# Windowed attention in fp32: the output stores moved onto the queue of the loads, with a reordered TensorE stage

## The chip, the cores and the metric

The kernel runs on one core of one Trainium2 chip. The metric is the device time of one execution in microseconds (us). TensorE is PE, VectorE DVE, ScalarE ACT, GpSimd POOL, SyncE SP. Transfers run on 16 DMA engines: in the traces the semaphore of each transfer of 128 partitions gets 16 completion counts, whether GpSimd or SP issued it. The time from the first to the last of the 16 is called the spread below; a large spread means that some DMA engines lag behind the others. A transfer issued by GpSimd goes onto GpSimd's queue (q0 in the profile), one issued by SP onto SP's (q1). The runs of a kernel scatter by about 1 us, so differences below half a microsecond are not read.

## The reference, cut to what matters

```python
B, S, D, W = 4, 4096, 1536, 64             # q, k, v: fp32, B x S x D
logits = einsum('bnwd,bnud->bnwu', q_w, k_w) * D ** -0.5   # in windows of 64 rows
attn = softmax(logits)
out  = einsum('bnwu,bnud->bnwd', attn, v_w)                # fp32
```

There are 16,384 rows of 1,536 numbers in each tensor. The core must read 302 MB and write 101 MB of HBM whatever it does on chip.

## The kernel before

Work goes in units of 256 rows: 63 of them, then two of 128. In a unit, partition p holds two consecutive rows of the tensor, so each partition's share of a transfer is one contiguous piece of 12,288 bytes. I call such a piece a row from here on. Loads are issued by GpSimd and cast fp32 to fp16 on the way; stores are issued by SP, but for the last few.

```python
    def load(u):
        for name, src in (("q", qf), ("k", kf), ("v", vf)):
            t = inp.tile([P, LR, D], FP16, tag=name + "16", name=name + "16")
            ...
            nc.gpsimd.dma_start(out=dst, in_=dram(src, u))
    ...
    def store(i):
        u = units[i]
        src = ...
        eng = nc.gpsimd if i >= N - PREFETCH - 2 else nc.sync
        eng.dma_start(out=dram(of, u), in_=src)

    prev = None
    for i, u in enumerate(units):
        if i + PREFETCH < N:               # PREFETCH = 3
            load(units[i + PREFETCH])
        for g in range(u.G):
            et = finish_scores(scores(u, g))
            if prev is not None:           # values one unit behind the scores
                pi, pg, pet = prev
                values(units[pi], pg, pet, False)
                ...
                    store(pi)
            prev = (i, g, et)
    ...
    values(units[pi], pg, pet, True)       # its three stores go to SP
```

`scores` transposes q and k on PE into PSUM and copies the result to SBUF (half the copies on DVE, half on ACT), then multiplies and exponentiates. `values` multiplies with v, and scales by the row sums while it evacuates PSUM into `out_sb`.

The build adds a limit: GpSimd's transfers share eight completion semaphores, so each waits for the eighth before it, and eight are in flight at most.

The softmax here doesn't subtract the row's maximum and nothing guards it: scores larger than these inputs give would overflow.

## Time and profile before

| | before |
|---|---|
| median of 4 runs | 958.65 us (958.32 to 959.07) |
| span of the profiled run | 956.8 us |
| first data packet starts, last ends | 2.6 us, 953.1 us |
| SP has seen every transfer complete | 953.6 us |
| GpSimd's final drain ends | 956.1 us |

Lines of the page of the kernel before. The first gives each engine's busy time, its share of the span and its instructions. The second has the busy share of the DMA engines in 40 slices, in tenths. Then come the queues with packets, MB and the time of their packets as a share of 16 engines' span, and the chain of waits that ended last, by engine.

```profile
PE 658.4 (69%) x5624; PEld 482.7 (50%) x5624; DVE 240.6 (25%) x392; ACT 456.1 (48%) x705; POOL 105.8 (11%) x204
...
DMA  9999999999999999999999999999999999999996
...
q0 software_dynamic: 28656, 156.51, 78.0%
q1 hardware_dynamic: 9072, 95.16, 24.0%
q8 instruction: 44, 0.72, 0.3%
...
HBM read 301.99 MB, written 100.66 MB: 421 GB/s over the span
...
DMA 86%; PE 8%; ACT 4%; issue 1%; DVE 0%; POOL 0%; ACTq 0%; POOLq 0%; DVEq 0%
```

No compute engine is near its limit, the DMA engines are busy in every slice, and the chain of waits runs through transfers. The shares of q0 and q1 add to over 100% because one packet's start overlaps the end of the one before. Loads count with their fp16 size in MB here; in HBM they are twice that.

The windows view of the kernel before: start and end in us, length, busy us of each engine (with instructions), granted PE clock, DMA share, GB/s.

```profile
100.00:500.00 400.00, 282.07 (x2373) 208.07 (x2371) 101.13 (x162) 191.78 (x298) 42.83 (x82) 0.87 1.03 267
500.00:900.00 400.00, 277.06 (x2382) 202.23 (x2380) 101.13 (x162) 192.31 (x298) 42.78 (x81) 0.89 1.03 267
925.00:940.00 15.00, 12.32 (x119) 8.68 (x118) 4.92 (x9) 9.37 (x15) 0.53 (x1) 0.94 0.99 267
940.00:957.00 17.00, 5.70 (x51) 3.12 (x49) 3.62 (x7) 7.03 (x12) 1.06 (x2) 0.81 0.61 250
```

A DMA share of 1.03 through the middle means that the engines are always busy. Each engine carries 2,048 rows.

```profile
SPq L257 <- PEq L257: 3.1, 2, 2.6
```

GpSimd issues its last store at 947.9 us. SP, having seen every transfer complete, waits 2.6 us longer at the closing barrier. The instruction records of the trace (not shown in the page's busy times) say for whom: a drain instruction of GpSimd that runs from 947.8 to 956.1 us.

### The profile page before, as it was taken

How to read it: one execution, taken by the hardware profiler on the slowest of the kernel's cores; microseconds unless marked ns; L12 is line 12 of the kernel's file. 1: busy time of each engine (PE TensorE's matmuls, PEld its weight loads, DVE VectorE, ACT ScalarE, POOL GpSimd, SP SyncE). 2: the span in 40 equal slices, each digit the busy share in tenths (PEclk: the TensorE clock that was granted, in tenths of full speed). 3: DMA queues.
4: the chain of work that ended last, by engine and by line, in shares of the span. 5: the costliest groups of instructions: out<-in, count | busy, mean ns of one | idle time of the engine just before them, and what ended most of it. 6: DMA issues, size and time to landing. Idle time of an engine off the chain costs nothing.

```text
span 956.8 us, 13110 instructions
## 1 busy us (share of the span) xinstructions
PE 658.4 (69%) x5624; PEld 482.7 (50%) x5624; DVE 240.6 (25%) x392; ACT 456.1 (48%) x705; POOL 105.8 (11%) x204
## 2 busy tenths in 40 slices
PE   4776766767767677676776766767667667676674
PEld 3454554645545555455464554555545445445452
DVE  1222222222222222222222222222222222222222
ACT  2544545444445454454545544445445444454445
POOL 3111011110110111101111011011110111111000
PEclk9978889888898898888978989889988999898888
DMA  9999999999999999999999999999999999999996
GB/s 185 242 268 263 275 269 258 279 258 269 270 256 279 257 270 279 250 277 267 259 280 255 271 272 255 279 259 269 279 252 275 266 261 279 257 269 273 253 252 268
DMA packets 37786, 252.51 MB, mean 264 GB/s; under 512 B 4192, under 2 KB 4192, under 8 KB 29664
## 3 DMA queue, kind: packets, MB, share of 16 engines
q0 software_dynamic: 28656, 156.51, 78.0%
q1 hardware_dynamic: 9072, 95.16, 24.0%
q8 instruction: 44, 0.72, 0.3%
q14 instruction: 14, 0.11, 0.0%
HBM read 301.99 MB, written 100.66 MB: 421 GB/s over the span
## 4 chain that ended last, share of the span: by engine, by line
DMA 86%; PE 8%; ACT 4%; issue 1%; DVE 0%; POOL 0%; ACTq 0%; POOLq 0%; DVEq 0%
DMA k<-in_k_dram 40%; DMA v<-in_v_dram 40%; DMA q<-in_q_dram 6%; PE tp L140 3%; PE lt L165 3%; ACT xt L147 2%; PE o L198 2%; ACT et L177 1%; ACT out_sb L204 1%; DVE xt L145 0%; PE lt L126 0%; PE sp L187 0%; POOL q L84 0%; ACTq L257 0%; POOL v L84 0%
## 5 line engine op out<-in xcount | busy, mean ns | idle before, releaser
L140 PE MATMUL tp<-ident,k 128*128 128x128 f16 x1536 | 259.6, 270 | 172.9 <-DMA k<-in_k_dram 172.9
L147 ACT COPY xt<-tp 128x1024 f16<-128x1024 f16 x192 | 194.3, 1012 | 348.3 <-PE tp L140 348.3
L140 PE MATMUL tp<-ident,q 128*128 128x128 f16 x1536 | 253.6, 264 | 52.1 <-ACT xt L147 21.4
L140 PEld LDWEIGHTS <-k 128*128 128x128 f16 x1536 | 156.8, 125 | 184.0 <-DMA k<-in_k_dram 183.8
L198 PE MATMUL o<-v,et 128*128 128x512 f16 x762 | 185.1, 378 | 61.5 <-ACT out_sb L204 61.4
L145 DVE COPY xt<-tp 128x1024 f16<-128x1024 f16 x192 | 132.7, 691 | 346.5 <-PE tp L140 346.5
L140 PEld LDWEIGHTS <-q 128*128 128x128 f16 x1536 | 163.0, 120 | 97.3 <-issue 67.6
L165 PE MATMUL lt<-xt 128*128 128x256 f16 x1512 | 188.4, 277 | 0.5
L204 ACT ACTIVATE out_sb<-o,rs 128x512 f32<-128x512 f32 x256 | 168.9, 686 | 19.0 <-PE o L198 11.1
L165 PEld LDWEIGHTS <-xt 128*128 128x128 f16 x1512 | 144.6, 100 | 31.2 <-ACT xt L147 13.8
L177 ACT ACTIVATE et<-lt,zeros 32x128 f16<-32x128 f32 (+1 forms) x256 | 91.8, 358 | 124.5 <-PE sp L187 114.6
L198 PEld LDWEIGHTS <-et 128*128 128x128 f16 x762 | 69.0, 96 | 146.9 <-issue 79.2
L206 DVE TENSOR_SCALAR out_sb<-o,rs 128x512 f32<-128x512 f32 x128 | 96.1, 750 | 151.4 <-PE o L198 151.4
L84 POOL DMA_DIRECT2D v<-in_v_dram x65 | 34.4, 529 | 343.1 <-PE o L198 309.9
L84 POOL DMA_DIRECT2D k<-in_k_dram x65 | 34.5, 531 | 332.4 <-DMA v<-in_v_dram 332.4
L192 DVE RECIPROCAL rs<-sp 128x2 f32<-128x2 f32 (+1 forms) x65 | 11.1, 170 | 209.1 <-PE sp L187 209.1
L84 POOL DMA_DIRECT2D q<-in_q_dram x65 | 34.6, 532 | 141.6 <-DMA k<-in_k_dram 140.8
L187 PEld LDWEIGHTS <-et 128*128 128x128 f16 x254 | 15.7, 97 | 1.9 <-ACT et L177 0.5
L187 PE MATMUL sp<-ones,et 128*128 128x1 f16 x254 | 15.6, 164 | 0.1
L216 POOL DMA_DIRECT2D out_dram<-out_sb x4 | 2.1, 532 | 25.2 <-ACT out_sb L204 22.3
L126 PE MATMUL lt<-xt 128*128 128x128 f16 x24 | 2.4, 221 | 2.6 <-ACT xt L147 1.7
L126 PEld LDWEIGHTS <-xt 128*128 128x128 f16 x24 | 1.4, 98 | 3.3 <-ACT xt L147 2.0
(10 smaller groups left out, 3.0 us busy)
## 6 DMA issues: line engine op xcount, KB each, us to landing
out_dram<-out_sb SPq DMA_DIRECT2D x60, 1536.0 KB, 11.4
q<-in_q_dram POOLq DMA_DIRECT2D x63, 768.0 KB, 40.4
k<-in_k_dram POOLq DMA_DIRECT2D x63, 768.0 KB, 38.1
v<-in_v_dram POOLq DMA_DIRECT2D x63, 768.0 KB, 38.0
out_dram<-out_sb POOLq DMA_DIRECT2D x3, 1536.0 KB, 9.1
q<-in_q_dram POOLq DMA_DIRECT2D x2, 384.0 KB, 30.3
k<-in_k_dram POOLq DMA_DIRECT2D x2, 384.0 KB, 26.2
v<-in_v_dram POOLq DMA_DIRECT2D x2, 384.0 KB, 21.9
```

The lines of the kernel that those rows point to most:

```text
L84: nc.gpsimd.dma_start(out=dst, in_=dram(src, u))
L126: nc.tensor.matmul(lv[:, r, :, :], lhsT=xt[:, c, 1, r, :], rhs=xt[:, c, 0, :R, :], start=(c == 0), stop=(c == DC - 1),)
L140: nc.tensor.transpose(tp[:, c - c0, x, r, :], src[:, g * R + r, c * P : (c + 1) * P], ident)
L145: nc.vector.tensor_copy(out=dst, in_=tp)
L147: nc.scalar.copy(out=dst, in_=tp)
L165: nc.tensor.matmul(lv[:, r, :, :], lhsT=xt[:, c, 1, r, :], rhs=xt[:, c, 0, :R, :], start=(c == 0), stop=(c == DC - 1),)
L177: nc.scalar.activation(et[s, :, :, s], lv[s, :, :, s], EXP, bias=zeros[s], scale=scale)
L187: nc.tensor.matmul(sp[:, t, 0:1], lhsT=et[:, r, t, :], rhs=ones[:, 0:1], start=(r == 0), stop=(r == R - 1),)
L192: nc.vector.reciprocal(out=rs, in_=sp[:, :, 0])
L198: nc.tensor.matmul(o, lhsT=et[:, r, t, :], rhs=u.v[:, g * R + r, sl], start=(r == 0), stop=(r == R - 1),)
L204: nc.scalar.activation(dst, o, COPY, bias=0.0, scale=rs[:, t : t + 1])
L206: nc.vector.tensor_scalar_mul(dst, o, scalar1=rs[:, t : t + 1])
```

## The change

Its intent is to have loads and stores pass in one order through one queue, to let the q transposes run while k still loads, to run the values right behind the scores, and to give the transposes three PSUM buffers. The core of the diff:

```diff
-    tp_ps = ...tile_pool(name="tp_ps", bufs=2, ...)
-    lt_ps = ...tile_pool(name="lt_ps", bufs=2, ...)
+    tp_ps = ...tile_pool(name="tp_ps", bufs=3, ...)
+    lt_ps = ...tile_pool(name="lt_ps", bufs=1, ...)
...
-        for c0 in range(0, DC, per):           # q and k of a chunk together
-            ... transpose q and k; copy by DVE and ACT in turn
+        for c0 in starts:
+            transpose(u.q, xq, c0, nc.vector.tensor_copy)
+        for i, c0 in enumerate(starts):
+            transpose(u.k, xk, c0, nc.scalar.copy if i == 1 else nc.vector.tensor_copy)
+            if i > 0:
+                product(starts[i - 1])
+        product(starts[-1])
...
-                if j % 2 == 0:                 # evacuation: 4 by ACT, 2 by DVE
+                if n % 2 == 0:                 # 3 by ACT, 3 by DVE
...
-        eng = nc.gpsimd if i >= N - PREFETCH - 2 else nc.sync
-        eng.dma_start(out=dram(of, u), in_=src)
+        for a, b in parts:
+            nc.gpsimd.dma_start(out=dram(of, u)[a:b], in_=src[a:b])
...
+        et = scores(u)
+        values(u, et, i == N - 1)
+        if i == N - 8:                         # one store in four pieces
+            src = u.o[0:8, : u.R, :]
+            dst = of[u.row0 : u.row0 + 8 * u.R].rearrange("(p r) d -> p r d", r=u.R)
+            for r in range(u.R):
+                nc.gpsimd.dma_start(out=dst[:, r, :], in_=src[:, r, :])
+            store(u, ((8, 16), (16, P)))
+        elif i < N - 1:
+            store(u)
```

The last unit's three stores stay on SP.

More of the change, by code (lines that the diff above doesn't have):

```diff
@@ L17, with __init__ @@
 class Unit:
-    def __init__(self, row0, G, R):
-        self.row0, self.G, self.R = row0, G, R
-        self.rows = P * G * R
+    def __init__(self, row0, R):
+        self.row0, self.R = row0, R
+        self.rows = P * R
 def plan(total):
-    tail = [(1, 1), (1, 1)]
+    tail = [1, 1]
     units, row = [], 0
-    body = total - sum(P * g * r for g, r in tail)
+    body = total - P * sum(tail)
     while row < body:
-        units.append(Unit(row, BODY_G, BODY_R))
+        units.append(Unit(row, 2))
         row += units[-1].rows
-    for g, r in tail:
-        units.append(Unit(row, g, r))
+    for R in tail:
+        units.append(Unit(row, R))
         row += units[-1].rows
@@ L37, in plan @@
     return units
-BODY_G, BODY_R = 1, 2
-PREFETCH = 3
+AHEAD = 3
 @with_exitstack
@@ L57 @@
     scale = float(D) ** -0.5
-    LR = BODY_G * BODY_R
+    RM = 2
     qf, kf, vf, of = (x.rearrange("b s d -> (b s) d") for x in (q, k, v, out))
@@ L64 @@
     consts = ctx.enter_context(tc.tile_pool(name="consts", bufs=1))
-    inp = ctx.enter_context(tc.tile_pool(name="inp", bufs=PREFETCH + 1))
+    inp = ctx.enter_context(tc.tile_pool(name="inp", bufs=AHEAD + 1))
     xtp = ctx.enter_context(tc.tile_pool(name="xtp", bufs=2))
@@ L68 @@
     rsp = ctx.enter_context(tc.tile_pool(name="rsp", bufs=4))
-    tp_ps = ctx.enter_context(tc.tile_pool(name="tp_ps", bufs=2, space=bass.MemoryType.PSUM))
-    lt_ps = ctx.enter_context(tc.tile_pool(name="lt_ps", bufs=2, space=bass.MemoryType.PSUM))
+    tp_ps = ctx.enter_context(tc.tile_pool(name="tp_ps", bufs=3, space=bass.MemoryType.PSUM))
+    lt_ps = ctx.enter_context(tc.tile_pool(name="lt_ps", bufs=1, space=bass.MemoryType.PSUM))
     o_ps = ctx.enter_context(tc.tile_pool(name="o_ps", bufs=3, space=bass.MemoryType.PSUM))
@@ L74, in dram, with load, load_all @@
     def dram(x, u):
-        rows = x[u.row0 : u.row0 + u.rows]
-        return rows.rearrange("(g p r) d -> p g (r d)", g=u.G, p=P, r=u.R)
+        return x[u.row0 : u.row0 + u.rows].rearrange("(p r) d -> p (r d)", p=P, r=u.R)
     ctx.enter_context(tc.manual_schedule())
-    def load(u):
-        for name, src in (("q", qf), ("k", kf), ("v", vf)):
-            t = inp.tile([P, LR, D], FP16, tag=name + "16", name=name + "16")
-            dst = t[:, : u.G * u.R, :].rearrange("p (g r) d -> p g (r d)", g=u.G)
-            nc.gpsimd.dma_start(out=dst, in_=dram(src, u))
-            setattr(u, name, t)
-    load(units[0])
+    def load(u, name):
+        src = {"q": qf, "k": kf, "v": vf}[name]
+        t = inp.tile([P, RM, D], FP16, tag=name + "16", name=name + "16")
+        dst = t[:, : u.R, :].rearrange("p r d -> p (r d)")
+        nc.gpsimd.dma_start(out=dst, in_=dram(src, u))
+        setattr(u, name, t)
+    def load_all(u):
+        for name in "qkv":
+            load(u, name)
+    load_all(units[0])
     ident = consts.tile([P, P], FP16, name="ident")
@@ L103 @@
     )
-    for u in units[1:PREFETCH]:
-        load(u)
+    for u in units[1:AHEAD]:
+        load_all(u)
     ets = {}
@@ L113, with scores @@
     turn = {R: 0 for R in ets}
-    flip = [0]
-    def scores(u, g):
+    def scores(u):
         R = u.R
-        per = 8 // (2 * R)
-        xt = xtp.tile([P, DC, 2, LR, P], FP16, tag="xt", name="xt")
+        CG = 4 if R == 2 else 6
+        xq = xtp.tile([P, DC, RM, P], FP16, tag="xq", name="xq")
+        xk = xtp.tile([P, DC, RM, P], FP16, tag="xk", name="xk")
         lt = lt_ps.tile([P, 512], FP32, tag="lt", name="lt")
         lv = lt[:, : R * R * P].rearrange("p (r s e) -> p r s e", r=R, s=R)
-        def mm(c):
-            for r in range(R):
-                nc.tensor.matmul(
-                    lv[:, r, :, :],
-                    lhsT=xt[:, c, 1, r, :],
-                    rhs=xt[:, c, 0, :R, :],
-                    start=(c == 0),
-                    stop=(c == DC - 1),
-                )
-        done = []
-        for c0 in range(0, DC, per):
-            tp = tp_ps.tile([P, per, 2, R, P], FP16, tag="tp", name="tp")
-            for c in range(c0, c0 + per):
-                for x, src in enumerate((u.q, u.k)):
-                    for r in range(R):
-                        nc.tensor.transpose(
-                            tp[:, c - c0, x, r, :], src[:, g * R + r, c * P : (c + 1) * P], ident
-                        )
-            dst = xt[:, c0 : c0 + per, :, :R, :]
-            if flip[0] % 2 == 0:
-                nc.vector.tensor_copy(out=dst, in_=tp)
-            else:
-                nc.scalar.copy(out=dst, in_=tp)
-            flip[0] += 1
-            done.append(range(c0, c0 + per))
-            if R == 1 and len(done) > 1:
-                for c in done.pop(0):
-                    mm(c)
-        return u, g, xt, lt, lv, mm, done
@@ L155, in finish_scores, with transpose @@
-    def finish_scores(state):
-        u, g, xt, lt, lv, mm, done = state
-        R = u.R
-        if R == 1:
-            for cs in done:
-                for c in cs:
-                    mm(c)
-        else:
-            for r in range(R):
-                for c in range(DC):
+        def transpose(src, xt, c0, copy):
+            tp = tp_ps.tile([P, CG, R, P], FP16, tag="tp", name="tp")
+            for c in range(c0, c0 + CG):
+                for r in range(R):
+                    nc.tensor.transpose(tp[:, c - c0, r, :], src[:, r, c * P : (c + 1) * P], ident)
+            copy(out=xt[:, c0 : c0 + CG, :R, :], in_=tp)
@@ L165, in finish_scores, with product @@
+        def product(c0):
+            for c in range(c0, c0 + CG):
+                for r in range(R):
                     nc.tensor.matmul(
                         lv[:, r, :, :],
-                        lhsT=xt[:, c, 1, r, :],
-                        rhs=xt[:, c, 0, :R, :],
-                        start=(c == 0),
+                        lhsT=xk[:, c, r, :],
+                        rhs=xq[:, c, :R, :],
+                        start=(c == 0 and r == 0),
                         stop=(c == DC - 1),
+                        skip_group_check=True,
@@ L171, in finish_scores @@
                     )
+        starts = list(range(0, DC, CG))
+        for c0 in starts:
[5 more added lines that the diff above has]
+        product(starts[-1])
         et = ets[R][turn[R] % 2]
@@ L178, in finish_scores, with values @@
         return et
-    def values(u, g, et, last):
+    def values(u, et, last):
         R = u.R
-        if not hasattr(u, "o"):
-            u.o = outp.tile([P, LR, D], FP32, tag="out_sb", name="out_sb")
+        u.o = outp.tile([P, RM, D], FP32, tag="out_sb", name="out_sb")
         sp = s_ps.tile([P, R, 2], FP32, tag="sp", name="sp")
@@ L192, in values @@
         nc.vector.reciprocal(out=rs, in_=sp[:, :, 0])
+        n = 0
         for t in range(R):
@@ L198, in values @@
                     nc.tensor.matmul(
-                        o, lhsT=et[:, r, t, :], rhs=u.v[:, g * R + r, sl],
+                        o, lhsT=et[:, r, t, :], rhs=u.v[:, r, sl],
                         start=(r == 0), stop=(r == R - 1),
                     )
-                dst = u.o[:, g * R + t, sl]
-                if j % 2 == 0:
+                dst = u.o[:, t, sl]
+                if n % 2 == 0:
                     nc.scalar.activation(dst, o, COPY, bias=0.0, scale=rs[:, t : t + 1])
@@ L206, in values, with store @@
                     nc.vector.tensor_scalar_mul(dst, o, scalar1=rs[:, t : t + 1])
+                n += 1
                 if last:
-                    nc.sync.dma_start(
-                        out=of[u.row0 : u.row0 + u.rows, sl], in_=u.o[:, 0, sl]
-                    )
-    def store(i):
-        u = units[i]
-        src = u.o[:, : u.G * u.R, :].rearrange("p (g r) d -> p g (r d)", g=u.G)
-        eng = nc.gpsimd if i >= N - PREFETCH - 2 else nc.sync
-        eng.dma_start(out=dram(of, u), in_=src)
-    prev = None
-    for i, u in enumerate(units):
-        if i + PREFETCH < N:
-            load(units[i + PREFETCH])
-        for g in range(u.G):
-            et = finish_scores(scores(u, g))
-            if prev is not None:
-                pi, pg, pet = prev
-                values(units[pi], pg, pet, False)
-                if pg == units[pi].G - 1:
-                    store(pi)
-            prev = (i, g, et)
-    pi, pg, pet = prev
-    values(units[pi], pg, pet, True)
+                    nc.sync.dma_start(out=of[u.row0 : u.row0 + u.rows, sl], in_=u.o[:, 0, sl])
+    def store(u, parts=((0, P),)):
+        src = u.o[:, : u.R, :].rearrange("p r d -> p (r d)")
+        for a, b in parts:
+            nc.gpsimd.dma_start(out=dram(of, u)[a:b], in_=src[a:b])
+    for i, u in enumerate(units):
+        if i + AHEAD < N:
+            load_all(units[i + AHEAD])
+        et = scores(u)
[8 more added lines that the diff above has]
+            store(u)
 _INS = ['q', 'k', 'v']
```

## The prediction

> **What bounds the kernel now.** The transfers, everywhere. The windows view gives a DMA share of 1.03 in each stretch from 25 to 925 us; PE is busy 69% of the span, ACT 48%, DVE 25% (busy table). The chain of waits is 86% DMA. Loads read 302 MB of HBM, stores write 101 MB. In the packet records a 12,288-byte row takes 474 ns in a load, 473 in a store; counted per engine the pace is one row per 460 ns from 60 to 900 us (427 GB/s), and 459 ns from 5 to 36 us, when loads run alone on one queue: two queues are neither faster nor slower than one. The Trainium skill puts the fabric ceiling at 435 GB/s (DMA: Bandwidth & Descriptors, Specifications). 2,048 rows per engine make 942 us of the 956.8 us span; the first packet starts at 2.6 us, the last ends at 953.1 us.
>
> The other 8 us are unequal engines. Each transfer's 16 completion counts spread 0.7 us at the start, 6.8 us at the end: about eight engines fall behind, which fits 44 instruction packets of 16 KB (0.93 us each) plus 19 smaller ones, 48 us of engine time, on half the engines. The slow ones work without a gap to the end: loads land on them at 938.1 us, the next stores at 941.8, 945.4 and 949.3 us, each 3.7 us after the one before. The DMA dips after 935 us are fast engines only.
>
> **What the change does.**
> - Stores move to GpSimd's queue: same bytes, rows and 16 engines (same page, "Issuing engines are not separate DMA queues"). 60 more issues of 0.53 us on POOL, hidden. About 0.
> - GpSimd's transfers share eight completion semaphores: eight in flight, two units, 29 us of work. A store waits for its values, and later loads stand behind it; that wait may last 18 us after the unit's v landed, and values should take 8. No stall.
> - Values right behind scores: PE waits about 1.9 us per unit for the exponentials (4 x 0.37 us and handoffs). PE per unit: transposes 3 to 5 us, products 3, values 3.2, waits 3: 12 to 14 us, against a transfer period of 14.7. Slack shrinks; time unchanged.
> - q transposed early, three buffers, copies 5:1 to DVE (0.69 against 1.01 us), evacuations 3:3: off the critical path.
> - Tail: three stores (9.2 us) stand queued behind the last load, covering the last unit's 6 to 7 us of compute. Slow engines stay gapless, as before.
> - The odd split of one store moves up to two rows (0.9 us) between halves of the engines: about -0.5 us if the lucky way. PE's instruction count is the same, so the imbalance stays.
>
> **Prediction.** 957.2 us, range 953.5 to 960.0. Faster by over 2%: 0.01; within 2%: 0.96; slower by over 2%: 0.03.
>
> **Right if** the DMA share stays 1.03 in the middle, rows stay at 459 to 461 ns, the completion spread still grows to 6 or 7 us, and the chain of waits is still over 80% DMA.
>
> **Wrong if** the single queue stalls at a store's completion before the next load (0.5 us each would add 30 us, a share below 1.0); if PE exceeds 14.7 us per unit, so POOL waits on out_sb with DMA idle; or if stores in blocks change the row pace (1% is 9 us). Gains above 5 us would need a smaller spread between engines.

## More of the kernel before

The end of the kernel before: the timeline of POOL (start, duration, what, idle time before it and its releaser), then SP's waits (total us, times, longest us).

```profile
936.37 0.53 POOL L216 DMA_DIRECT2D out_dram<-out_sb  x1 [11.90 <-ACT out_sb L204]
942.59 0.53 POOL L216 DMA_DIRECT2D out_dram<-out_sb  x1 [5.68 <-ACT out_sb L204]
947.86 0.53 POOL L216 DMA_DIRECT2D out_dram<-out_sb  x1 [4.74 <-ACT out_sb L204]
```

## The result, and the profile after

| | before | after |
|---|---|---|
| median of 4 runs | 958.65 us | 953.35 us (952.92 to 954.11) |
| span of the profiled run | 956.8 us | 952.2 us |
| engine time per row, 60 to 900 us | 461.4 ns | 459.3 ns |
| last data packet ends | 953.1 us | 950.4 us |
| SP has seen every transfer complete | 953.6 us | 950.9 us |
| GpSimd's final drain ends | 956.1 us | 951.5 us |

The ratio of the times is 0.9945, with a 95% interval of 0.9928 to 0.9963. Engine time per row is the stretch of 840 us times 16 engines, over the 12,288-byte rows whose packets ended in it.

Of the 4.6 us between the two profiled spans, 2.7 us lie before the last data packet ends, and 1.9 us after it.

The lines of the page after that answer to those of before:

```profile
PE 629.0 (66%) x5624; PEld 430.1 (45%) x5624; DVE 363.6 (38%) x584; ACT 291.0 (31%) x515; POOL 139.8 (15%) x267
...
DMA  9999999999999999999999999999999999999997
...
q0 software_dynamic: 37376, 250.89, 101.9%
q8 instruction: 44, 0.72, 0.3%
q1 hardware_dynamic: 432, 0.79, 0.2%
...
HBM read 301.99 MB, written 100.66 MB: 423 GB/s over the span
```

All of the store traffic went from q1 to q0, and the two queues' summed packet time went from 102.0% of the span to 102.1% of a shorter one, that is, it fell by about 4 us (1.020 x 956.8 is 975.9 us; 1.021 x 952.2 is 972.2 us). ACT fell from 456 to 291 us and DVE rose from 241 to 364 us. The chain of waits of the changed kernel breaks off after five short pieces in this profile, so it says nothing either way.

The windows view after:

```profile
100.00:500.00 400.00, 267.48 (x2380) 182.44 (x2380) 154.20 (x244) 122.20 (x217) 57.36 (x108) 0.92 1.03 268
500.00:900.00 400.00, 268.35 (x2389) 183.59 (x2387) 153.46 (x244) 121.81 (x216) 59.17 (x112) 0.92 1.03 269
925.00:940.00 15.00, 9.90 (x86) 6.50 (x86) 6.41 (x12) 5.42 (x10) 1.61 (x3) 0.86 1.04 328
940.00:957.00 17.00, 2.52 (x12) 0.87 (x10) 0.92 (x2) 2.47 (x5) 0.00 (x0) 0.58 0.33 134
```

The share is still 1.03 in the middle: no stall, and the same saturation. GB/s rose from 267 to 268 or 269, half a per cent, which is the whole effect on the middle and is easy to overlook. The end, again POOL's timeline and SP's wait at the barrier:

```profile
929.78 0.54 POOL L196 DMA_DIRECT2D out_dram<-out_sb  x1 [3.74 <-DVE xq L131]
934.42 0.53 POOL L196 DMA_DIRECT2D out_dram<-out_sb  x1 [4.10 <-ACT out_sb L186]
```

```profile
SPq L236 <- PEq L236: 1.2, 2, 0.8
```

The last GpSimd store is issued 13 us earlier, and SP waits 0.8 us for the others at the barrier, where it was 2.6.

To see where a row got cheaper, I cut 60 to 900 us into bins of 1 us, and sorted them by the share of store rows among the rows in flight:

```
share of store rows     before, ns a row (bins)     after, ns a row (bins)
under 0.02              459.6 (382)                 458.6 (307)
0.02 to 0.2             460.5 (54)                  459.8 (120)
0.2 to 0.4              462.0 (35)                  459.6 (128)
0.4 to 0.6              463.5 (351)                 460.1 (217)
0.6 to 0.98             463.8 (18)                  459.8 (60)
least-squares fit       load row 458.2              load row 457.6
                        store row 465.6             store row 459.0
                        instruction packet 760      instruction packet 772
```

While loads run alone the kernels differ by 1.0 ns a row, and by 0.6 in the fit, which takes the instruction packets out. While stores and loads share the engines, the kernel before pays about 3.4 ns a row more. In the kernel before that happens on two queues, in the changed one on one.

The packet records show the same without bins or a fit. From 60 to 900 us a store packet was recorded at 472.1 ns on average in the kernel before and at 462.2 ns in the changed one; a load packet at 474.0 and 474.3. Stores are a quarter of the rows, so 9.9 ns on each are about 2.5 ns on the mean row; the pace fell by 2.1.

### The profile page after: what moved, and what is told of

Same layout as the page of the kernel before. It is cut to its first block, busy times and chain, and to the rows that moved or that the text cites. A ratio compares the mean times of both kernels' runs of the same rounds, so it can differ in the third digit from the quotient of the medians.

```text
span 952.2 us, 13234 instructions
## 1 busy us (share of the span) xinstructions
PE 629.0 (66%) x5624; PEld 430.1 (45%) x5624; DVE 363.6 (38%) x584; ACT 291.0 (31%) x515; POOL 139.8 (15%) x267
## 5 line engine op out<-in xcount | busy, mean ns | idle before, releaser
L136 PE MATMUL lt<-xq,xk 128*128 128x256 f16 (+1 forms) x1536 | 228.9, 305 | 19.8 <-DVE xk L131 19.4
L130 PE MATMUL tp<-ident,k 128*128 128x128 f16 x1536 | 132.1, 247 | 128.1 <-DMA k<-in_k_dram 127.1
L136 PEld LDWEIGHTS <-xk 128*128 128x128 f16 x1536 | 154.8, 109 | 69.3 <-DVE xk L131 40.9
L131 DVE COPY xk<-tp 128x1024 f16<-128x1024 f16 (+1 forms) x128 | 88.2, 689 | 253.4 <-PE tp L130 253.4
L130 PEld LDWEIGHTS <-k 128*128 128x128 f16 x1536 | 113.8, 113 | 144.6 <-DMA k<-in_k_dram 139.3
L131 ACT COPY xk<-tp 128x1024 f16<-128x1024 f16 (+1 forms) x65 | 65.4, 1006 | 354.3 <-PE tp L130 354.3
L188 DVE TENSOR_SCALAR out_sb<-o,rs 128x512 f32<-128x512 f32 x191 | 143.4, 751 | 69.0 <-PE o L180 68.9
L131 DVE COPY xq<-tp 128x1024 f16<-128x1024 f16 (+1 forms) x193 | 121.4, 681 | 54.1 <-PE tp L130 53.2
L130 PE MATMUL tp<-ident,q 128*128 128x128 f16 x1536 | 100.7, 224 | 60.1 <-DMA q<-in_q_dram 59.6
L130 PEld LDWEIGHTS <-q 128*128 128x128 f16 x1536 | 89.5, 100 | 89.8 <-DMA q<-in_q_dram 88.6
## 6 DMA issues: line engine op xcount, KB each, us to landing
q<-in_q_dram POOLq DMA_DIRECT2D x63, 768.0 KB, 28.8
k<-in_k_dram POOLq DMA_DIRECT2D x63, 768.0 KB, 28.8
v<-in_v_dram POOLq DMA_DIRECT2D x63, 768.0 KB, 28.8
```

The lines of the kernel that those rows point to most:

```text
L130: nc.tensor.transpose(tp[:, c - c0, r, :], src[:, r, c * P : (c + 1) * P], ident)
L131: copy(out=xt[:, c0 : c0 + CG, :R, :], in_=tp)
L136: nc.tensor.matmul(lv[:, r, :, :], lhsT=xk[:, c, r, :], rhs=xq[:, c, :R, :], start=(c == 0 and r == 0), stop=(c == DC - 1), skip_group_che ...
L188: nc.vector.tensor_scalar_mul(dst, o, scalar1=rs[:, t : t + 1])
```

## The experiments

Two theories for the pace. **A**: an engine that takes turns between two queues loses time. **B**: the pace changed because compute changed (copies moved from ACT to DVE, PE's order). And **C**, for the end: GpSimd's final drain, not the last transfer, ends the program. The table gives the numbers that all the full-size runs are judged by; the e kernels ran in one job, a and b in another, f1 in a third, each beside its own runs of the kernel before (medians 958.62, 958.71 and 958.72 us). The four columns on the right are of each kernel's profiled run.

| run | median, us | ns a row, 60 to 900 us | last packet ends | SP saw all done | drain ends | span |
|---|---|---|---|---|---|---|
| before | 958.65 | 461.4 | 953.1 | 953.6 | 956.1 | 956.8 |
| after | 953.35 | 459.3 | 950.4 | 950.9 | 951.5 | 952.2 |
| e1 | 954.20 | 459.5 | 950.4 | 950.9 | 951.7 | 952.5 |
| e2 | 958.74 | 461.4 | 953.1 | 953.7 | 956.3 | 957.0 |
| e3 | 953.95 | 459.5 | 949.9 | 950.4 | 951.0 | 951.8 |
| e4 | 956.44 | 461.4 | 953.1 | 953.9 | 948.3 | 954.7 |
| a1 | 953.39 | 459.4 | 949.3 | 949.8 | 950.4 | 951.1 |
| a2 | 953.59 | 459.4 | 949.6 | 950.1 | 950.7 | 951.4 |
| b1 | 954.25 | 459.4 | 951.5 | 952.0 | 950.3 | 952.7 |
| b2 | 957.37 | 459.6 | 952.7 | 953.3 | 951.7 | 954.1 |
| f1 | 955.43 | 459.8 | 951.9 | 952.4 | 952.9 | 953.7 |

### e1: the kernel before, with only its stores moved

```diff
-        eng = nc.gpsimd if i >= N - PREFETCH - 2 else nc.sync
+        eng = nc.gpsimd
```

> The kernel before, its one difference that every store but the last unit's three goes to GpSimd's queue. Theory A (two queues taking turns cost time: a store row costs 465.6 ns of an engine's time in the kernel before and 459.0 ns after, fitted over 1 us bins): store rows fall to about 459 ns, the pace to 458.5 ns a row, the last packet ends at 949 to 951 us instead of 953.1, the time falls by 3 to 5 us, to 953.5 to 955.5. Theory B (the pace changed because copies moved from ACT to DVE and the order of PE's work changed): store rows stay at 465 ns and the time within 1 us of before, 958.5.

Measured: 954.20 us, ratio 0.9951 (0.9938 to 0.9963). The pace is 459.5 ns, and the fit gives 457.7 ns for a store row. Its ACT and DVE times, from its page, are those of before:

```profile
PE 653.6 (69%) x5624; PEld 476.4 (50%) x5624; DVE 240.8 (25%) x392; ACT 456.1 (48%) x705; POOL 137.9 (14%) x264
...
q0 software_dynamic: 37296, 250.89, 101.9%
```

This one line of the change, without any of the compute part, brings 4.4 of the 5.3 us. Theory B does not explain that. The other 0.9 us is not pinned down: e3, below, has the whole compute part too and was only 0.25 us faster than e1 in the same job. (The paces expected of e1 and e2 counted instruction packets as rows. On that count e1 had 458.6 ns and e2 460.6.)

### e2: the changed kernel, with its stores back on SP

```diff
+        eng = nc.gpsimd if units.index(u) >= N - 5 else nc.sync
-            nc.gpsimd.dma_start(out=dram(of, u)[a:b], in_=src[a:b])
+            eng.dma_start(out=dram(of, u)[a:b], in_=src[a:b])
```

The store in four pieces was also made one.

> The changed kernel without the odd split and with its stores on SP's queue but for those of the last five units, as before. Theory A: store rows cost about 465 ns again, the pace is 460 to 460.5 ns, and the time is that of before within 1.5 us, 957 to 959. Theory B: 953 to 954.

Measured: 958.74 us, ratio 1.0000 (0.9988 to 1.0013); store rows cost 466.2 ns in the fit. Its page shows the queues of before beside the compute of the changed kernel:

```profile
PE 622.8 (65%) x5624; PEld 427.5 (45%) x5624; DVE 362.2 (38%) x584; ACT 290.6 (30%) x515; POOL 105.7 (11%) x204
...
q0 software_dynamic: 28656, 156.51, 78.0%
q1 hardware_dynamic: 9072, 95.16, 24.0%
```

SP's wait at the barrier is back as well:

```profile
SPq L231 <- PEq L231: 3.3, 2, 2.8
```

With two queues again, the whole gain is gone, the part at the end included. The compute part of the change (early q transposes, values behind scores, three buffers, other shares for ACT and DVE) is worth nothing that these runs resolve.

### e3 and a2: the changed kernel with the split store in one piece

```diff
-        if i == N - 8:
-            ...                                # the four pieces
-        elif i < N - 1:
+        if i < N - 1:
             store(u)
```

> The changed kernel with the store of the eighth unit from the end in one piece. If the split balances the engines, as its form suggests: 0.5 us slower than the changed kernel, 953.9. From the completion counts, which show six of the slow engines relieved by 0.6 us but the two slowest loaded by 0.5 to 0.9 us: 0.3 to 0.9 us faster, 952.4 to 953.1.

> The changed kernel once more, beside the next three on one chip: 953.4 us within 0.6. Its completion counts should again end with a spread of 8.5 to 9.5 us, and GpSimd's drain 2 to 4 us after the last transfer of its queue.

> The changed kernel without the odd split, now beside the changed kernel on one chip. In its first run it took 953.95 us, against 953.35 for the changed kernel in another job. If the split helps: 0.4 to 0.8 us slower than a1. If it does nothing, the two agree within 0.3 us.

Measured: 953.95 us alone (e3). Beside the changed kernel in one job: 953.59 us without the split (a2) and 953.39 with it (a1), ratios to before 0.9950 and 0.9945, with intervals that overlap widely. The means differ by 0.37 us. Both have the sign that the split helps, against what I read out of one profile's completion counts, but the runs don't prove it. It is worth at most about half a microsecond. One expectation for a1 failed: its spread at the last load was 7.7 us and not 8.5 to 9.5.

### e4: the kernel before, with its last four stores on SP as well

```diff
-        eng = nc.gpsimd if i >= N - PREFETCH - 2 else nc.sync
+        eng = nc.sync
```

> The kernel before with its last four stores on SP's queue like the other 60. In the kernel before GpSimd's final drain begins with its last transfer at 947.8 us and ends at 956.1 us, 2.4 us after SP has seen every transfer complete (953.6 us). Theory C (the drain of GpSimd's queue, 8.2 us from the last issue, ends the program): with the last GpSimd transfer issued at about 921 us, the program ends about 1.3 us after SP's last completion, 1.5 to 2 us earlier: 956.5 to 957.2. Rival (the end follows the last transfer by a fixed time whichever queue it was on): 958 to 959.

Measured: 956.44 us, ratio 0.9976 (0.9962 to 0.9990). The last packet ends at 953.1 us as before, and still the program ends 2.1 us sooner, since the drain is over at 948.3 us. SP's longest wait at the barrier fell from 2.6 to 0.5 us:

```profile
SPq L257 <- PEq L257: 0.7, 2, 0.5
```

So theory C holds: in the kernel before, GpSimd's drain ended the program, and its wait was worth about 2 us. One detail of my expectation was wrong. The drain does not take a fixed 8.2 us from the last issue (17.1 us in the changed kernel). It ends after the last packet of GpSimd's queue, by 2.2 to 2.5 us in after, e1, e3, a1, a2, b1, b2, f1 and m1, by 4.0 to 4.4 us in before, e2, e4 and m2, and by 1.1 us in m3. In the full-size kernels the longer lag goes with the stores on SP's queue, but in m1 and m2 it is the other way round. What makes it one or the other is open.

### m1 and m2: transfers alone, on two queues and on one

These kernels only transfer. Their outputs are wrong, which doesn't matter for the times.

```python
    for i in range(24):            # A: loads (GpSimd) beside stores
        load()
        store(nc.sync, sa)         # m2: nc.gpsimd
    ...
    for i in range(24):            # B: loads alone
        t = load()
    nc.vector.tensor_copy(out=sb, in_=t)
    for i in range(20):            # C: stores alone, after B
        store(nc.sync, sb)         # m2: nc.gpsimd
    ...                            # D: 20 stores, SP and ACT in turn, after C
```

> Transfers alone, no TensorE work, a wrong result on purpose. Stage A: 24 loads on GpSimd's queue beside 24 stores on SP's; B: 24 loads alone; C: 20 stores alone on SP's; D: 20 stores, alternately on SP's and ACT's queue. Taking turns between queues is the cost: A 462 to 464 ns a row, B and C 457 to 459, D 460 to 464. Descriptors made in hardware are the cost: A 461 to 463, C and D both 464 to 466. Also, if instruction fetches for PE make the engines unequal, the spread of a transfer's 16 completion counts stays under 1.5 us to the end, since there is no PE code to fetch.

> The same with the stores of A and C on GpSimd's queue, loads and stores in turn. Both theories: A 457.5 to 459.5 ns a row, B and C 457 to 459; D as in m1.

Measured, in ns of engine time per row (B from 190 to 268 us, C from 285 to 340, D from 365 to 425; in C and D a packet that a window cuts counts in part):

```
                                m1: stores on SP    m2: stores on GpSimd
A, loads and stores, 20 to 180  462.0               462.5
A, the part from 100 to 180     462.1               457.8
B, loads alone                  458.0               457.8
C, stores alone                 463.0               468.3
D, stores on SP and ACT         463.3               463.6
```

The windows view of the two, two parts of stage A and then B, m1 first (this view has DVE and POOL busy, clock, DMA share, GB/s):

```profile
20.00:90.00 70.00, 0.00 (x0) 4.75 (x9) 1.00 1.03 319
100.00:180.00 80.00, 0.00 (x0) 5.81 (x11) 1.00 1.03 319
190.00:268.00 78.00, 0.12 (x1) 7.91 (x15) 1.00 1.04 215
```

```profile
20.00:90.00 70.00, 0.00 (x0) 9.57 (x18) 1.00 1.03 312
100.00:180.00 80.00, 0.00 (x0) 11.70 (x22) 1.00 1.03 322
190.00:268.00 78.00, 0.00 (x0) 8.07 (x16) 1.00 1.04 215
```

Once m2 has settled, stage A shows the effect without any compute: 319 against 322 GB/s, 4.3 ns a row. Over the whole stage it does not: until 90 us m2 ran slower and unevenly, which I can't explain, and the window from 100 us was chosen after seeing that. So e1 and e2 carry the claim, and stage A only agrees with it in part.

Neither theory foretold C and D. Stores alone on GpSimd's queue were slower than on SP's and not faster, which speaks against the idea that SP's queue is slow in itself. Stores in turn on the queues of SP and ACT took no longer than on SP's alone (463.3 and 463.0), so taking turns did not cost time between every two queues. Long runs of stores alone are slower than loads alone on either queue, for a reason that these runs do not show, and that may hide a cost of turns in D.

The last forecast, a spread under 1.5 us without PE code, failed too. In m1 the loads' spread was 1.4 to 1.8 us in A and about 1.0 in B. In m2 it grew to 4.1 us by 97 us and stayed there, although its page has no packet on q8, where the full-size kernels have their 44, and a single small instruction packet. Fetches are thus not the only thing that makes engines lag.

### m3: which kind of turn costs time

```python
    for i in range(20):            # A: loads on two queues, no stores
        load()                     #    GpSimd, cast to fp16
        g = load32()               #    SP, plain fp32
    for i in range(16):            # B: SP's loads alone
        g = load32()
    ...                            # C to F: GpSimd's queue, 32-partition loads and stores,
                                   # one by one (C, E) or by fours (D, F)
```

> Transfers alone, a wrong result on purpose, to tell what in two queues costs time. m1 and m2 gave 462.1 ns a row for loads and stores on two queues and 457.9 for the same on one, but 463 and 468 for stores alone on SP's or GpSimd's queue, so hardware-made descriptors are not the cost. Stage A: loads alone on two queues (casting ones on GpSimd's, plain fp32 ones on SP's), B: plain loads on SP's queue alone. C and E: GpSimd's queue alone, two rows of each engine at a time, load and store in turn; D and F: the same transfers, four loads, then four stores. If taking turns between queues costs time: A 461 to 463, B 458, C and E equal to D and F within 0.5 ns. If changing between a load row and a store row on an engine costs time (about 4 ns a change): A and B both 458, C and E 1 to 2 ns a row above D and F.

Measured: A 461.6 ns a row from 20 to 140 us; B 459.8 ns from 160 to 200 us. With m1's 458.0 for the casting loads alone, the mean of the two kinds alone is 458.9, so two queues cost 2.7 ns a row though both only loaded. B is short and not level: from 170 to 200 us it ran at 461.1 ns, and with that figure the cost is 2.1 ns. The packet records point the same way: SP's loads were recorded at 471.3 ns on average in A, and at 462.9 in B. That speaks for the two queues and not for the direction as the cause, for part of the effect at least; that taking turns is how they cost time is the likeliest reading and is not shown. A rival was not tested: in the kernel before a GpSimd load landed 38 to 40 us after its issue, in the changed one 28.8 us after it, so more work was in flight at once. C to F failed as a test: with 32-partition transfers every stage ran at 473 to 635 ns a row and wavered by more than the few ns in question. Whether changes between load and store add to it is open.

### b1: the last GpSimd stores moved to SP, against the drain

```diff
+            eng = nc.sync if units.index(u) >= N - 3 else nc.gpsimd
-            nc.gpsimd.dma_start(out=dram(of, u)[a:b], in_=src[a:b])
+            eng.dma_start(out=dram(of, u)[a:b], in_=src[a:b])
```

> The changed kernel with the stores of the third and second unit from the end on SP's queue as well. Drain theory: the last transfer of GpSimd's queue lands at about 943 us instead of 949.4, its drain ends by 947, and the program ends 0.2 to 0.4 us after SP's last completion plus the barriers of 0.7 us: 0.5 to 1 us faster than a1. If the drain does not matter: equal to a1 or, since the queues take turns in the tail again, up to 0.3 us slower.

Measured: 954.25 us, 0.9 us slower than a1. The drain did end early (950.3 us, before SP's last completion at 952.0), but the last packet ended 2.2 us later than in a1. Stores on SP's queue take turns with the last unit's loads where on GpSimd's they stand behind them: the last v landed at 944.6 us, against 938.5 in a1, and the last compute came so much later. The 16 counts of the first of the last unit's stores lie within 0.2 us of each other (4.3 us in a1): all engines, the slow ones too, had by this sign run out of work and were waiting for it. The kernel before ends in the same way (0.2 us). The miss is worth keeping: in the tail, one queue is also an order.

### b2: rows moved between engines

```diff
         if i == N - 8:
-            ...                                # the four pieces
+            store(u, [(p, p + 8) for p in range(0, 64, 8)], nc.sync)
+            store(u, ((64, P),))
```

> As b1, without the odd split, and with half of the store of the eighth unit from the end (64 partitions) in eight SP transfers of 8 partitions, which eight engines alone should carry, the lowest by the Trainium skill: eight engines get 12 rows and eight get 4 where each had 8. If the engines that lag are the other eight: their lag behind the fastest falls by about 3.7 us and the time by up to 1.8 us against b1. If the ones that lag are these eight: spread and time grow by as much. If the laggards are spread over both halves: the spread hardly falls and the time rises by up to 1.8 us.

The page meant is DMA: Bandwidth & Descriptors, section "Why a DMA increments its semaphore by 16 and not by 1". The trace agrees in part: each of the eight transfers brought 9 semaphore updates, not 16; which engines carried it the trace does not show.

Measured: 957.37 us (five runs from 955.87 to 959.16), 3.1 us slower than b1. The spread of a load's 16 completion counts (the loads issued from 900 to 908 us) rose from 8.0 to 11.0 us. That refutes the first case, in which the lagging engines are the other eight. It does not tell the other two apart: spread and time grew as in the second, the time by more than either allowed. So it stays open in which half the lagging engines lie. No version beat the changed kernel.

### f1: more instructions for PE

```diff
-        for t in range(R):                     # row sums, on PE
+        for again in range(8):
+          for t in range(R):
```

> The changed kernel with the row-sum matmuls done eight times over (the result is the same): 31% more PE instructions, off the critical path, since PE is busy 66%. If instruction fetches for PE make the engines unequal: about 58 fetch packets of 16 KB instead of 44, the spread of the completion counts at the end grows from 8 or 9 us to 10 to 12, and the time rises by 1 to 3 us, to 954.5 to 956.5. If the lag has another source: 953.4 within 0.6.

Measured: 955.43 us, ratio 0.9967 (0.9953 to 0.9980), 2.0 us above the changed kernel's two medians. The page has exactly the fetch packets that were expected:

```profile
q8 instruction: 58, 0.95, 0.4%
```

The spread of the last load's 16 completion counts grew to 10.8 us, from 8.9 (after) and 7.7 (a1). The Trainium skill (Runtime: NRT & Kernel Launch, Instruction fetch mechanics) says that each engine's sequencer refills its instruction memory over a DMA queue in blocks of 16 KiB, 256 instructions. The 5,624 matmuls and 5,624 weight loads of PE then make 43.9 blocks, and the trace has 44 packets. The page calls their cost "mostly hidden". In this kernel, which is bound by its transfers, it is not. A block's packet is recorded at 0.94 us on average; the fit above mixes it with packets of 8 KB, and with the two apart it gives 970 ns for a block and 330 for the smaller ones (after). Fourteen blocks more are then 13.6 us of engine time, or 0.85 us on the mean of 16 engines. That is close to what the pace cost: it rose by 0.5 ns a row, or 0.9 us (load and store rows cost nearly the same in the fit as after, 457.6 and 458.8 ns). The rest came with the larger spread. That the engines which get more blocks finish last is inferred: the trace does not tell which engine fetched what.

## Why the prediction was right or wrong

The prediction was 957.2 us, with a range from 953.5 to 960.0; the measured 953.35 lies just below it. The class (within 2%) was right; the expected gain of 1.4 us was a fourth of the measured 5.3.

- **"Two queues are neither faster nor slower than one", and for the move of the stores "About 0": wrong, and the step that failed.** Moving the stores, alone, brought 4.4 us (e1), and undoing it took everything away (e2). The number was in the trace: 461.4 ns against 459.3. I had 460 and 459, because I had counted the bytes of the instruction packets as rows in the long stretch, and then I called 1 ns nothing, although 2,048 rows make 2 us of it. Sorting the stretch by whether stores were in flight, as done above, would have shown 459.6 against 463.5 ns before any run. The prediction did name this way of being wrong ("if stores in blocks change the row pace"), but gave it no weight.
- **The end of the program: missing from the sum.** I took it to follow the last packet by a fixed time. GpSimd's drain added 2.4 us after SP's last completion in the kernel before, and adds 0.6 us in the changed one. e4 gets 2.2 us from that alone. In the changed kernel GpSimd's last packet ended 2.6 us earlier, as everything did, and the drain followed it after 2.4 us instead of 4.4. That shorter lag is the 1.9 us after the last packet. It came with the stores' move (e1 has it, e2 does not); why the lag is shorter is open.
- The two terms are 2.7 us (before the last packet) and 1.9 us (after it) in the profiles of before and after. The pace alone would give 2.1 ns x 2,048 rows = 4.4 us on the mean engine. The slowest engine got less of it, since the spread at the last load grew from 6.8 to 8.9 us; in a1 it was 7.7 us, and there the last packet ended 3.8 us before that of the kernel before. Why it grew is not settled. In the full-size runs it was 6.8 and 7.3 us with the stores on SP's queue (before, e2) and 7.7 to 8.9 with one queue and the same PE code (after, a1, a2, e1, e3). The prediction said that gains above 5 us would need a smaller spread; the gain was 5.3 us with a larger one.
- **Transfers bound the kernel, no stall from one queue, eight transfers in flight are enough: right.** The share stayed 1.03, and issue to landing is 28.8 us for each kind of load, the 29 us foretold.
- **PE's order, buffers, copies and evacuations are off the critical path: right** (e2, ratio 1.0000).
- **Unequal engines: right; their source: right in part.** With more instruction fetches in f1 the spread and the time grew, as they had to. But fetches are not the only source (m2), and "the imbalance stays" was wrong: the spread should "still grow to 6 or 7 us", and it grew to 7.7 (a1) and 8.9 (after).
- **The split store, "about -0.5 us": not refuted, not proven** (a1, a2: 0.2 us between medians).
- **The tail's three stores behind the last load: right**, and b1 shows what happens without the order. "Slow engines stay gapless, as before" was wrong of the kernel before, where the 16 counts of the last unit's first store lie within 0.2 us; in the changed kernel they lie 4.3 us apart.

## What to carry to other kernels

When a kernel is bound by its DMA engines, count the engine time per row, multiply a difference of one nanosecond by the number of rows before calling it nothing, and compare stretches with one queue in use against stretches with two. Here stretches with loads and stores mixed ran 0.7% faster on one queue than on two (463.5 and 460.1 ns a row), with eight transfers in flight and no wait of a store that ran the queue dry. Look at what happens after the last packet too, since a queue's final drain can end the program, and count instruction fetches as traffic.

## What the Trainium skill lacked or had wrong

- DMA: Bandwidth & Descriptors, "Issuing engines are not separate DMA queues" and "Rules for kernel authors": they say that transfers issued by several engines interleave on the same 16 engines and that spreading them does not help. They lack that it can cost: with only the stores moved from SP's queue to that of the loads, a row went from 461.4 to 459.5 ns and the kernel from 958.62 to 954.20 us (e1). Loads alone took 461.6 ns on two queues and 458.0 or 459.8 on either (m1, m3).
- No page that I found has GpSimd's final drain: in the full-size kernels it ended 2.2 to 2.5 or 4.0 to 4.4 us after the last packet of GpSimd's queue, and taking it off the end of the kernel before made that 2.2 us faster (e4).
- Runtime: NRT & Kernel Launch, "Instruction fetch mechanics": the block size agrees (44 packets for 11,248 instructions), but "mostly hidden" lacks the cost to a transfer-bound kernel: 0.94 us of a DMA engine for each block by the packet records, and 2.0 us more for 14 blocks more (f1).
- DMA: Bandwidth & Descriptors, "Specifications": nothing is wrong here; the fabric ceiling of 435 GB/s is not contradicted. Loads alone, at 457.8 ns for 12,288 bytes of HBM (m2), make 429 GB/s on 16 engines.
